# Gate and up products of a SwiGLU layer by Strassen's method: seven products for eight

## The chip, the cores and the metric

The kernel runs on 1 core of one Trainium2 chip. The metric is the device time of one execution in microseconds, the median of several runs. A profiled execution of the same kernel gives the trace. PE is TensorE (matmuls), DVE is VectorE, ACT is ScalarE, POOL is GpSimd, and SP is the engine whose queue issues the DMAs.

## The reference

A decoder block on 256 tokens with 2048 channels: two token mixers, merged, and then a dense SwiGLU layer with 5632 hidden columns. All is float32. Cut to what matters here:

```python
def reference(x, ...):
    h = _rms_norm(x, attn_norm)
    ...                                        # two mixers, merge, output projection
    x = x + mix @ w_out
    h2 = _rms_norm(x, ffn_norm)
    x = x + (jax.nn.silu(h2 @ w_gate) * (h2 @ w_up)) @ w_down
```

h2 is 256 x 2048, w_gate and w_up are 2048 x 5632, w_down is 5632 x 2048.

## The kernel before

Every large product is done in float32 precision with three matmuls. An operand is split in two: hi is its copy in the rounded type float32r (ACT, L107 or in the helper hilo), lo is what is missing (DVE subtracts hi from the value, L108 or in hilo). A product is then hi x hi + hi x lo + lo x hi (L122 to L124); a matmul takes a 128x128 stationary piece of the activation and 512 moving columns of the weight.

load_pair brings two k-tiles of a weight, 512 columns wide (a raw tile of 128x1024, 512 KB, in one DMA from SP's queue; the pool has four raw buffers), and splits it into whi and wlo (three buffers each). chunk_tok does one block of 512 columns: for each pair of k-tiles two k-tiles x two token tiles x three matmuls, 12 in all, into one PSUM bank per token tile; then it calls an evacuation. It is a generator: run steps it, and after each pair pumps a side task, if there is one.

The SwiGLU part goes over eleven column blocks (L1065 to L1067). For each, a gate chunk (8 pairs, 96 matmuls) is evacuated by evac_gate: silu of the product times the row's norm factor rs2 (ACT). Then comes an up chunk, evacuated by evac_up: product times rs2 times the silu (DVE, L1058), then four transposes on PE per token tile (transpose_hilo, L183) and a split of the transposed activation into act, which stays in SBUF. The norm's gain is already in h2T, its row factor rs2 is applied at the evacuations. Then w_down is streamed: four chunks of 44 k-tiles, with act as the stationary operand.

The order of the instructions on each engine is the tile framework's: it traces the program, orders by priority and an estimate of time, and sets the semaphores. A split of a later pair can so stand ahead of an evacuation that the program names first. Each engine works its own queue in order. Of POOL's work before, the select on Q (L712, 128x1024, one operand) and the small powers (L381) are mentioned below; Q and N belong to the delta rule mixer, where DVE also does small subtractions (L707, L708).

Of the kernel before, what the change touches and what calls it, by code (L numbers as in the profile page):

```python
# [16 lines left out]
P = 128  # L17
S = 256
# [25 lines left out]
def tile_hybrid_block(  # L44
# [36 lines left out]
    big = ctx.enter_context(tc.tile_pool(name="big", bufs=4))  # L81
    dram = ctx.enter_context(tc.tile_pool(name="dram", bufs=2, space=bass.MemoryType.DRAM))
    psm = ctx.enter_context(tc.tile_pool(name="psm", bufs=4, space=bass.MemoryType.PSUM))
    pss = ctx.enter_context(tc.tile_pool(name="pss", bufs=4, space=bass.MemoryType.PSUM))

# [10 lines left out]
    def sps():  # L96
        return pss.tile([P, 512], F32, tag="sd", name=nm("sd"))
# [81 lines left out]
    def transpose_hilo(src4, hi, lo, k0, t):  # L179
        """src4: four [P, P] pieces of a token-major tile, to k-tiles k0..k0+3 of hi and lo."""  # L180
# [112 lines left out]
    def narrow():  # L293
# [29 lines left out]
        # softplus(a) = max(a, 0) + log1p(exp(-|a|)), the log1p as 2 artanh(e / (2 + e))  # L323
# [9 lines left out]
        # the argument is at most 1/3, so terms to s^15 reach float32  # L333
# [53 lines left out]
    def normed_T(pst, hi, lo, gcol):  # L387
        """rms-norm of four heads side by side, transposed, times a gain by channel"""
# [209 lines left out]
    # merge-gate logits and the product of branch A wait in DRAM for the merge  # L598
# [46 lines left out]
    def conv_silu(st, ps, base, silu_out):  # L645
        """short causal convolution of four heads by channel, then silu"""
# [30 lines left out]
    # one-hot columns for the blocks' inverses: lane = 32 * column group + problem  # L677
# [8 lines left out]
    def gdn_prep(st, hg):  # L686
        """what hangs on the decay alone"""
# [52 lines left out]
    def gdn_q(st, hg):  # L740
# [22 lines left out]
        # the 32 x 32 blocks on the diagonal, a problem and eight of its columns to a lane  # L763
# [237 lines left out]
    fin = ctx.enter_context(tc.tile_pool(name="fin", bufs=1))  # L1001
    gain2 = fin.tile([P, D], F32, name="gain2", tag="gain2")
# [4 lines left out]
    x2 = fin.tile([P, NT, D], F32, name="x2")  # L1007
# [4 lines left out]
    ss2 = fin.tile([P, NT, 4], F32, name="ss2")  # L1012
# [17 lines left out]
    act = [[], []]  # L1030
    for q in range(2):
        for i in range(3):
            if i == 2:
                act[q].append(fin.tile([P, 12, S], F32R, name=f"act{q}{i}"))
            elif i == 1:
                act[q].append(fin.tile([P, 16, S], F32R, name=f"act{q}{i}"))
            else:
                act[q].append(big_tile(f"act{q}{i}", F32R))
    rs2 = fin.tile([P, NT], F32, name="rs2")
    sst = fin.tile([P, NT], F32, name="sst")  # L1040
# [7 lines left out]
    def evac_gate(c):
        def f(t, ps):
            sg[t] = fin.tile([P, 512], F32, tag="tmp", name=nm("sg"), bufs=6)  # L1050
            nc.scalar.activation(sg[t], ps, AF.Silu, scale=rs2[:, t : t + 1])

        return f

    def evac_up(c):
        def f(t, ps):
            a = sg[t]
            nc.vector.scalar_tensor_tensor(a, ps, rs2[:, t : t + 1], a, ALU.mult, ALU.mult)  # L1058
            k0 = 4 * c
            transpose_hilo(  # L1060
                [a[:, i * P : (i + 1) * P] for i in range(4)], act[0][k0 // 16], act[1][k0 // 16], k0 % 16, t
            )

        return f
# [51 lines left out]
```

## Time and profile before

| | us |
|---|---|
| median of 3 runs | 1974.59 |
| lowest, highest | 1973.98, 1975.04 |
| span of the profiled execution, first to last instruction | 1971.1 |
| PE busy in the span | 1946.4 |
| DVE, ACT, POOL busy | 1155.0, 928.4, 54.1 |

The span is that of one profiled execution; the runs' time also has what lies around it. Busy times count the time in which at least one instruction of an engine is under way. Matmuls overlap each other in the trace, so the duration of one is longer than the distance to the next. The weights that are streamed come to 355.76 MB read from HBM.

### The profile page before, as it was taken

Reading aid. Unit: us, or ns where it says so; the run is one execution under the profiler, and the core shown is the slowest. Engines: PE = TensorE matmul, PEld = TensorE weight load, DVE = VectorE, ACT = ScalarE, POOL = GpSimd, SP = SyncE. Lnnn points to the kernel's source line nnn. Section 1 sums busy time; section 2 is a strip of 40 time slices with the busy share of each in tenths; the row PEclk is TensorE's granted clock in tenths of the full one; section 3 lists DMA queues with packets and bytes.
Section 4 is the critical chain, followed back from the end, with each engine's and each line's share of the span. In section 5 each row is a group of like instructions: output and inputs, shape, how many; then the busy total and the mean of one; then the engine's idle time right before and its main releaser. Section 6 shows DMA issues by size and latency. Waiting matters only on the chain.

```text
span 1971.1 us, 27260 instructions
## 1 busy us (share of the span) xinstructions
PE 1946.4 (99%) x10485; PEld 1651.0 (84%) x10485; DVE 1155.0 (59%) x1715; ACT 928.4 (47%) x1377; POOL 54.1 (3%) x97
## 2 busy tenths in 40 slices
PE   8999999999999999999999999999999999999999
PEld 6878877876998998999987788888888888888887
DVE  5555766655468587687774665554455444544443
ACT  5434555555454554654543544444444444443333
POOL 0001000001000000100100000000000000000000
PEclk9999999999999999999999999999999999999999
DMA  8566545546767566566574965666666666656663
GB/s 231 170 183 193 161 129 162 170 149 200 217 173 203 169 178 198 158 193 166 153 200 157 333 201 183 191 192 183 191 191 186 191 191 191 191 185 201 201 202 130
DMA packets 207605, 367.04 MB, mean 186 GB/s; under 512 B 25473, under 2 KB 34546, under 8 KB 207090
## 3 DMA queue, kind: packets, MB, share of 16 engines
q1 hardware_dynamic: 207442, 365.28, 62.1%
q8 instruction: 82, 1.34, 0.3%
q14 instruction: 49, 0.40, 0.1%
q10 hardware_dynamic: 32, 0.01, 0.0%
HBM read 355.76 MB, written 9.45 MB: 185 GB/s over the span
## 4 chain that ended last, share of the span: by engine, by line
PE 96%; DMA 2%; DVE 1%; ACT 0%; SPq 0%; issue 0%; POOL 0%; ACTq 0%; POOLq 0%; DVEq 0%
PE mm L123 25%; PE mm L124 24%; PE mm L122 24%; PE mm L141 4%; PE mm L143 4%; PE mm L142 4%; PE sd L183 1%; PE sd L668 1%; PE sd L448 1%; PE sd L561 1%; DMA Q<-grow_d 1%; PE sd L748 1%; DMA raw<-in_w_branch_b_dram 1%; PE sd L567 1%; PE sd L568 0%; PE sd L267 0%
## 5 line engine op out<-in xcount | busy, mean ns | idle before, releaser
L108 DVE TENSOR_TENSOR wlo<-raw,whi 128x1024 fp32r<-128x1024 f32 x632 | 773.7, 1225 | 658.5 <-ACT whi L107 656.1
L107 ACT ACTIVATE whi<-raw 128x1024 fp32r<-128x1024 f32 x632 | 669.7, 1060 | 804.5 <-PE mm L124 674.4
L123 PE MATMUL mm<-wlo,hT_hi 128*128 128x512 f32 x704 | 276.7, 393 | 0.0
L124 PE MATMUL mm<-whi,hT_lo 128*128 128x512 f32 x704 | 276.5, 393 | 0.0
L124 PE MATMUL mm<-whi,h2T_lo 128*128 128x512 f32 x704 | 274.0, 389 | 0.0
L123 PE MATMUL mm<-wlo,h2T_hi 128*128 128x512 f32 x704 | 273.9, 389 | 0.0
L122 PE MATMUL mm<-whi,hT_hi 128*128 128x512 f32 x704 | 260.2, 393 | 0.0
L122 PE MATMUL mm<-whi,h2T_hi 128*128 128x512 f32 x704 | 249.9, 390 | 0.0
L143 PE MATMUL mm<-hT_hi,wlo 128*128 128x256 f32 x768 | 218.4, 285 | 0.0
L141 PE MATMUL mm<-hT_hi,whi 128*128 128x256 f32 x768 | 218.4, 285 | 0.0
L142 PE MATMUL mm<-hT_lo,whi 128*128 128x256 f32 x768 | 218.3, 284 | 0.0
L124 PEld LDWEIGHTS mm<-whi,hT_lo 128*128 128x128 f32 x704 | 132.3, 188 | 27.7 <-issue 1.1
L123 PEld LDWEIGHTS mm<-wlo,hT_hi 128*128 128x128 f32 x704 | 132.3, 188 | 27.5 <-issue 1.1
L124 PEld LDWEIGHTS mm<-whi,h2T_lo 128*128 128x128 f32 x704 | 132.2, 188 | 27.5
L122 PEld LDWEIGHTS mm<-whi,h2T_hi 128*128 128x128 f32 x704 | 132.2, 188 | 27.1
L123 PEld LDWEIGHTS mm<-wlo,h2T_hi 128*128 128x128 f32 x704 | 132.2, 188 | 27.0
L122 PEld LDWEIGHTS mm<-whi,hT_hi 128*128 128x128 f32 x704 | 132.1, 188 | 26.3 <-issue 0.2
L141 PEld LDWEIGHTS mm<-hT_hi,whi 128*128 128x128 f32 x768 | 147.2, 192 | 0.6
L142 PEld LDWEIGHTS mm<-hT_lo,whi 128*128 128x128 f32 x768 | 147.2, 192 | 0.2
L143 PEld LDWEIGHTS mm<-hT_hi,wlo 128*128 128x128 f32 x768 | 146.9, 192 | 0.4
L123 PE MATMUL mm<-wlo,act 128*128 128x512 f32 x352 | 138.5, 393 | 0.0
L124 PE MATMUL mm<-whi,act 128*128 128x512 f32 x352 | 138.4, 393 | 0.0
(288 smaller groups left out, 2247.7 us busy)
## 6 DMA issues: line engine op xcount, KB each, us to landing
raw<-in_w_in_dram SPq DMA_DIRECT2D x272, 512.0 KB, 3.7
raw<-in_w_gate_dram SPq DMA_DIRECT2D x88, 512.0 KB, 4.4
raw<-in_w_up_dram SPq DMA_DIRECT2D x88, 512.0 KB, 3.7
raw<-in_w_down_dram SPq DMA_DIRECT2D x88, 512.0 KB, 4.7
raw<-in_w_branch_a_dram SPq DMA_DIRECT2D x32, 512.0 KB, 4.7
raw<-in_w_branch_b_dram SPq DMA_DIRECT2D x32, 512.0 KB, 4.9
raw<-in_w_out_dram SPq DMA_DIRECT2D x32, 512.0 KB, 4.7
wc<-in_w_cmp_dram SPq DMA_DIRECT2D x16, 256.0 KB, 4.2
```

Of the source, the lines that this page charges most:

```text
L107: nc.scalar.activation(hi[:, :, :width], raw[:, :, :width], AF.Copy)
L108: nc.vector.tensor_tensor(lo[:, :, :width], raw[:, :, :width], hi[:, :, :width].bitcast(F32), ALU.subtract)
L122: nc.tensor.matmul(o, lhsT=sh, rhs=hi[:, j, :width], start=kt == 0, stop=False)
L123: nc.tensor.matmul(o, lhsT=sh, rhs=lo[:, j, :width], start=False, stop=False)
L124: nc.tensor.matmul(o, lhsT=sl, rhs=hi[:, j, :width], start=False, stop=kt == kts - 1)
L141: nc.tensor.matmul(o, lhsT=hi[:, j, ws], rhs=xh[:, kt, :], start=first, stop=False, skip_group_check=True)
L142: nc.tensor.matmul(o, lhsT=hi[:, j, ws], rhs=xl[:, kt, :], start=False, stop=False, skip_group_check=True)
L143: nc.tensor.matmul(o, lhsT=lo[:, j, ws], rhs=xh[:, kt, :], start=False, stop=last, skip_group_check=True)
L183: nc.tensor.transpose(pt[:, i * P : (i + 1) * P], s4, ident)
L448: nc.tensor.matmul(pc[:60, :P], lhsT=kp[:, l0 + l, :], rhs=wc[:, l, :], start=l0 + l == 0, stop=l0 + l == 31)
L561: nc.tensor.transpose(pt[:n, r * P : (r + 1) * P], pb[:, r, c0 : c0 + n], ident)
L567: nc.tensor.matmul(po, lhsT=wh, rhs=ph[:n], start=i == 0, stop=False)
```

## The change

Of the eleven column blocks, block 0 stays as it was, except that its activation is written to DRAM (act_d) and not transposed at once. Blocks 1 to 10 compute gate and up together by Strassen's method (in the Winograd form): the activation is cut into halves by token tile and by k (k-tiles 0 to 7 and 8 to 15), which gives a 2x2 matrix of pieces; gate's and up's two k-halves form the other 2x2 matrix. Seven products M1 to M7 take the place of eight. Each product still takes three matmuls for the split operands, and a step j (k-tiles j and j+8 of both weights) has 7 x 3 = 21 matmuls where chunk_tok has 24. There are 8 steps in a block. Seven PSUM banks hold M1 to M7.

The sums of the activation's pieces (S1 to S4) and the row factor rs2 are prepared once, by the side task factors, while block 0 runs: sums and products on POOL, splits on ACT and DVE. The sums of weight pieces (ta and tb, two 512-wide additions each) are made on POOL in every step and then split as the weights are. The seven products are put together at a block's end by DVE and ACT, silu and the product of gate and up included. Blocks 1 and 2 transpose their activation at once (act_r); the others write it to DRAM. During the first chunk of w_down the side task act_in reads it back, transposes and splits it. w_down's k-tiles are taken in the order of blocks 1, 2, 0, 3 to 10. PSUM and SBUF pools are closed and opened anew to make room.

```diff
--- before.py
+++ after.py
@@ -110,25 +124,26 @@
         )
         return hi, lo
 
-    def chunk_tok(w, c0, width, kts, stat, evac):
-        ps = [psm.tile([P, 512], F32, tag="mm", name=nm("mm")) for _ in range(NT)]
-        for k0 in range(0, kts, 2):
+    def chunk_tok(w, c0, width, kts, stat, evac, order=None):
+        ps = [mps() for _ in range(NT)]
+        pairs = order or list(range(0, kts, 2))
+        for n, k0 in enumerate(pairs):
             hi, lo = load_pair(w, k0, c0, width)
             for j in range(2):
-                kt = k0 + j
+                first, last = n + j == 0, j == 1 and n == len(pairs) - 1
                 for t in range(NT):
-                    sh, sl = stat(kt, t)
+                    sh, sl = stat(k0 + j, t)
                     o = ps[t][:, :width]
-                    nc.tensor.matmul(o, lhsT=sh, rhs=hi[:, j, :width], start=kt == 0, stop=False)
+                    nc.tensor.matmul(o, lhsT=sh, rhs=hi[:, j, :width], start=first, stop=False)
                     nc.tensor.matmul(o, lhsT=sh, rhs=lo[:, j, :width], start=False, stop=False)
-                    nc.tensor.matmul(o, lhsT=sl, rhs=hi[:, j, :width], start=False, stop=kt == kts - 1)
+                    nc.tensor.matmul(o, lhsT=sl, rhs=hi[:, j, :width], start=False, stop=last)
             yield
         for t in range(NT):
             evac(t, ps[t])
         yield
...
-    fin = ctx.enter_context(tc.tile_pool(name="fin", bufs=1))
+    fin = ctx.enter_context(tc.tile_pool(name="fin", bufs=1, side="right"))
...
-    h2T_hi = big_tile("h2T_hi", F32R)
-    h2T_lo = big_tile("h2T_lo", F32R)
+    h2T_hi = hp.tile([P, KD, S], F32R, name="h2T_hi")
+    h2T_lo = hp.tile([P, KD, S], F32R, name="h2T_lo")
...
+    NB = DFF // 512
+    big_cm.__exit__(None, None, None)
...
+    act_d = dram.tile([NB, NT, P, 512], F32, name="act_d", bufs=1)
...
+    A12, A11, A22, S1, S3, S2, S4 = range(7)
+    Fh = [fac.tile([P, 7, 2, P], F32R, name=f"Fh{g}") for g in range(4)]
+    Fl = [fac.tile([P, 7, 2, P], F32R, name=f"Fl{g}") for g in range(4)]
+
+    def tmp(n):
+        return fin.tile([P, 512], F32, tag="tmp", name=nm(n), bufs=6)
+
+    def factors():
+        dg = tmp("dg")
+        for t in range(NT):
+            nc.vector.tensor_scalar_mul(dg[:, t * P : (t + 1) * P], ident, rs2[:, t : t + 1])
+        one = tmp("one")
+        nc.vector.memset(one[:, :P], 1.0)
+        pr = sps()
+        nc.tensor.matmul(pr[:, :S], lhsT=one[:, :P], rhs=dg[:, :S], start=True, stop=True)
+        nc.scalar.activation(rsrow, pr[:, :S], AF.Copy)
+        yield
+        hv = h2T_hi.bitcast(F32).rearrange("p (h k) s -> p h k s", h=2)
+        lv = h2T_lo.bitcast(F32).rearrange("p (h k) s -> p h k s", h=2)
+        for g in range(4):
+            js = slice(2 * g, 2 * g + 2)
+            q = sw.tile([P, 4, 2, P], F32, tag="T", name=nm("q"), bufs=2)
+            for t in range(NT):
+                ts = slice(t * P, (t + 1) * P)
+                qt = q[:, 2 * t : 2 * t + 2]
+                nc.gpsimd.tensor_tensor(qt, hv[:, :, js, ts], lv[:, :, js, ts], ALU.add)
+                qf = qt.rearrange("p h k c -> p (h k) c")
+                nc.gpsimd.tensor_tensor(qf, qf, rsrow[:, ts].unsqueeze(1).to_broadcast([P, 4, P]), ALU.mult)
+            yield
+            sm = sw.tile([P, 4, 2, P], F32, tag="T", name=nm("sm"), bufs=2)
+            nc.gpsimd.tensor_tensor(sm[:, 0], q[:, 3], q[:, 2], ALU.subtract)
+            nc.gpsimd.tensor_tensor(sm[:, 1], q[:, 1], q[:, 3], ALU.subtract)
+            nc.gpsimd.tensor_tensor(sm[:, 2], q[:, 1], sm[:, 0], ALU.subtract)
+            nc.gpsimd.tensor_tensor(sm[:, 3], q[:, 0], sm[:, 2], ALU.subtract)
+            hilo(Fh[g][:, 0:3], Fl[g][:, 0:3], q[:, 0:3])
+            hilo(Fh[g][:, 3:7], Fl[g][:, 3:7], sm)
+            yield
...
-    for c in range(DFF // 512):
-        run(chunk_tok(w_gate, c * 512, 512, KD, stat_h2, evac_gate(c)))
-        run(chunk_tok(w_up, c * 512, 512, KD, stat_h2, evac_up(c)))
+    def evac_gate(t, ps):
+        sg[t] = tmp("sg")
+        nc.scalar.activation(sg[t], ps, AF.Silu, scale=rs2[:, t : t + 1])
+
+    def evac_up(t, ps):
+        nc.vector.scalar_tensor_tensor(sg[t], ps, rs2[:, t : t + 1], sg[t], ALU.mult, ALU.mult)
+        nc.sync.dma_start(act_d[0, t], sg[t])
+
+    side.append(factors())
+    run(chunk_tok(w_gate, 0, 512, KD, stat_h2, evac_gate))
+    run(chunk_tok(w_up, 0, 512, KD, stat_h2, evac_up))
+    drain()
+    hp_cm.__exit__(None, None, None)
+    close_banks()
+
+
+    late = ctx.enter_context(tc.tile_pool(name="late", bufs=1, side="right", reuse_waits="tile"))
+    act_r = [late.tile([P, 8, S], F32R, name=f"act_r{q}") for q in range(2)]
+    pst_cm = tc.tile_pool(name="pst", bufs=1, space=bass.MemoryType.PSUM, reuse_waits="tile")
+    pst = pst_cm.__enter__()
+    halves = {
+        "g": w_gate.rearrange("(h j p) c -> j p h c", h=2, p=P),
+        "u": w_up.rearrange("(h j p) c -> j p h c", h=2, p=P),
+    }
+
+    def split(src, n, pool, tag, bufs):
+        hi = pool.tile([P, 2, 512], F32R, tag=tag[0], name=nm(tag[0]), bufs=bufs)
+        lo = pool.tile([P, 2, 512], F32R, tag=tag[1], name=nm(tag[1]), bufs=bufs)
+        hilo(hi[:, :n], lo[:, :n], src[:, :n])
+        return hi, lo
+
+    def strassen_step(j, c, M, order, first, last):
+        raw = {}
+        for n in ("g", "u"):
+            raw[n] = stream.tile([P, 2, 512], F32, tag="raw", name=nm("raw"))
+            nc.sync.dma_start(raw[n], halves[n][j][:, :, c * 512 : (c + 1) * 512])
+        b21, b11, b22, b12 = raw["g"][:, 0], raw["g"][:, 1], raw["u"][:, 0], raw["u"][:, 1]
+        ta = sw.tile([P, 2, 512], F32, tag="T", name=nm("ta"), bufs=2)
+        nc.gpsimd.tensor_tensor(ta[:, 0], b11, b12, ALU.add)
+        nc.gpsimd.tensor_tensor(ta[:, 1], b22, b12, ALU.add)
+        tb = sw.tile([P, 2, 512], F32, tag="T", name=nm("tb"), bufs=2)
+        nc.gpsimd.tensor_tensor(tb[:, 0], ta[:, 0], b22, ALU.add)
+        nc.gpsimd.tensor_tensor(tb[:, 1], tb[:, 0], b21, ALU.add)
+        gh, gl = split(raw["g"], 2, stream, ("whi", "wlo"), 3)
+        uh, ul = split(raw["u"], 1, stream, ("whi", "wlo"), 3)
+        ah, al = split(ta, 2, sw, ("thi", "tlo"), 3)
+        bh, bl = split(tb, 2, sw, ("thi", "tlo"), 3)
+        moving = {
+            1: (A11, gh[:, 1], gl[:, 1]),
+            2: (A12, gh[:, 0], gl[:, 0]),
+            3: (S4, uh[:, 0], ul[:, 0]),
+            4: (A22, bh[:, 1], bl[:, 1]),
+            5: (S1, ah[:, 0], al[:, 0]),
+            6: (S2, bh[:, 0], bl[:, 0]),
+            7: (S3, ah[:, 1], al[:, 1]),
+        }
+        for m in order:
+            f, hi, lo = moving[m]
+            fh, fl = Fh[j // 2][:, f, j % 2], Fl[j // 2][:, f, j % 2]
+            nc.tensor.matmul(M[m], lhsT=fh, rhs=hi, start=first, stop=False)
+            nc.tensor.matmul(M[m], lhsT=fh, rhs=lo, start=False, stop=False)
+            nc.tensor.matmul(M[m], lhsT=fl, rhs=hi, start=False, stop=last)
+
+    def strassen_block(c):
+        M = {m: pst.tile([P, 512], F32, tag="M", name=nm("M"), bufs=7) for m in range(1, 8)}
+        for j in range(8):
+            order = (1, 2, 3, 5, 7, 6, 4) if j < 7 else (6, 1, 5, 3, 7, 4, 2)
+            strassen_step(j, c, M, order, j == 0, j == 7)
+        m1, v, x, y = tmp("m1"), tmp("v"), tmp("x"), tmp("y")
+        nc.scalar.activation(m1, M[1], AF.Copy)
+        nc.vector.tensor_tensor(v, M[6], m1, ALU.subtract)
+        nc.vector.tensor_tensor(x, M[5], v, ALU.add)
+        nc.vector.tensor_tensor(x, M[3], x, ALU.add)
+        nc.vector.tensor_tensor(v, v, M[7], ALU.subtract)
+        nc.vector.tensor_tensor(y, M[4], v, ALU.subtract)
+        nc.vector.tensor_tensor(m1, M[2], m1, ALU.add)
+        nc.vector.tensor_tensor(v, M[5], v, ALU.add)
+        nc.scalar.activation(m1, m1, AF.Silu)
+        nc.scalar.activation(y, y, AF.Silu)
+        nc.vector.tensor_tensor(x, m1, x, ALU.mult)
+        nc.vector.tensor_tensor(y, y, v, ALU.mult)
+        for t, a in enumerate((x, y)):
+            if c > 2:
+                nc.sync.dma_start(act_d[c, t], a)
+                continue
+            pt = pst.tile([P, 512], F32, tag="tr", name=nm("tr"), bufs=1)
+            for i in range(4):
+                nc.tensor.transpose(pt[:, i * P : (i + 1) * P], a[:, i * P : (i + 1) * P], ident)
+            ks, ts = slice(4 * c - 4, 4 * c), slice(t * P, (t + 1) * P)
+            hilo(act_r[0][:, ks, ts], act_r[1][:, ks, ts], pt.rearrange("p (k c) -> p k c", k=4))
+
+    for c in range(1, NB):
+        strassen_block(c)
+    pst_cm.__exit__(None, None, None)
+    sw_cm.__exit__(None, None, None)
+    fac_cm.__exit__(None, None, None)
+    open_banks()
+    actp = ctx.enter_context(tc.tile_pool(name="actp", bufs=1, reuse_waits="tile"))
+    rest = [0] + list(range(3, NB))
+    act_l = {c: [actp.tile([P, 4, S], F32R, name=f"act{q}_{c}") for q in range(2)] for c in rest}
+
+    def act_in():
+        for c in rest:
+            for t in range(NT):
+                a = tmp("a")
+                nc.sync.dma_start(a, act_d[c, t])
+                transpose_hilo([a[:, i * P : (i + 1) * P] for i in range(4)], act_l[c][0], act_l[c][1], 0, t)
+            yield
...
+    order = [4 * c + k for c in [1, 2] + rest for k in (0, 2)]
+    side.append(act_in())
     for c in range(4):
-        run(chunk_tok(w_down, c * 512, 512, KF, stat_act, evac_down(c)))
+        run(chunk_tok(w_down, c * 512, 512, KF, stat_act, evac_down(c), order), 1)
+    close_banks()
```

## Rows read from the trace of the kernel before

**Rows 1.** The page's first part: busy us, share of the span, instructions.
```profile
PE 1946.4 (99%) x10485; PEld 1651.0 (84%) x10485; DVE 1155.0 (59%) x1715; ACT 928.4 (47%) x1377; POOL 54.1 (3%) x97
```

**Rows 2.** Stretches: engines' busy time, granted PE clock, DMA share.
```profile
core 0: us, PE busy (x) PEld busy (x) DVE busy (x) ACT busy (x) POOL busy (x), PEclk, DMA share, GB/s
1085.00:1090.00 5.00, 4.99 (x12) 3.92 (x13) 0.82 (x2) 1.06 (x1) 0.00 (x0) 0.50 0.83 272
1277.20:1721.50 444.30, 444.30 (x2002) 368.80 (x2001) 222.24 (x202) 193.22 (x200) 0.00 (x0) 1.00 0.64 190
```

**Rows 3.** Up evacuations, two per block: ns min/median/max, first and last start.
```profile
L1058 DVE SCALAR_TENSOR_TENSOR sg<-mm,rs,sg x21: 739/743/746, 1277.2 to 1721.5; 128x512 f32<-128x512 f32 x21
```

**Rows 4.** Largest waits, 1277.2 to 1721.5 us: us together, times, longest.
```profile
ACT whi L107 <- PE mm L124: 226.6, 140, 1.7
DVE wlo L108 <- ACT whi L107: 215.6, 161, 2.1
...
```

**Rows 5.** Timeline of DVE, a block's end: start, us, xN merged [idle before].
```profile
1362.18 1.23 DVE L108 TENSOR_TENSOR wlo<-raw,whi 128x1024 fp32r<-128x1024 f32 x1 [1.49 <-ACT whi L107]
1364.90 1.23 DVE L108 TENSOR_TENSOR wlo<-raw,whi 128x1024 fp32r<-128x1024 f32 x1 [1.49 <-ACT whi L107]
1366.05 1.40 DVE L1058 SCALAR_TENSOR_TENSOR sg<-mm,rs,sg 128x512 f32<-128x512 f32 x2
...
1372.37 1.29 DVE L177 TENSOR_TENSOR act<-sd,act 128x512 fp32r<-128x512 f32 x2 [0.80 <-ACT act L176]
```

**Rows 6.** Timeline of PE at the transposes behind that block.
```profile
1371.10 1.04 PE L183 MATMUL sd<-ident,sg 128*128 128x128 f32 x8
1371.89 0.48 PE L122 MATMUL mm<-whi,h2T_hi 128*128 128x512 f32 x1
```

**Rows 7.** Groups by line, 1277 to 1722 us: busy us, mean ns; idle before.
```profile
L177 DVE TENSOR_TENSOR act<-sd,act 128x512 fp32r<-128x512 f32 x20 | 12.9, 686 | 7.9 <-ACT act L176 7.9
L107 ACT ACTIVATE whi<-raw 128x1024 fp32r<-128x1024 f32 x161 | 170.7, 1061 | 228.7 <-PE mm L124 228.2
L176 ACT ACTIVATE act<-sd 128x512 fp32r<-128x512 f32 x20 | 10.9, 596 | 14.2 <-PE sd L183 14.2
```

**Rows 8.** Timeline of DVE: two splits on end, POOL idle.
```profile
292.76 2.35 DVE L108 TENSOR_TENSOR wlo<-raw,whi 128x1024 fp32r<-128x1024 f32 x2
```

**Rows 9.** POOL's select on Q, all four: ns min/median/max.
```profile
L712 POOL TENSOR_SCALAR_AFFINE_SELECT Q<-Q x4: 1096/1100/1961, 475.2 to 827.0; 128x1024 f32<-128x1024 f32 x4
```

**Rows 10.** Timeline of POOL and DVE, the select of 1.96 us.
```profile
827.01 1.96 POOL L712 TENSOR_SCALAR_AFFINE_SELECT Q<-Q 128x1024 f32<-128x1024 f32 x1 [5.03 <-ACT Q L711]
...
826.80 3.25 DVE L108 TENSOR_TENSOR wlo<-raw,whi 128x1024 fp32r<-128x1024 f32 x2
```

**Rows 11.** Timeline of POOL and DVE, a select of 1.10 us.
```profile
475.24 1.10 POOL L712 TENSOR_SCALAR_AFFINE_SELECT Q<-Q 128x1024 f32<-128x1024 f32 x1 [9.99 <-ACT esc L715]
...
474.90 0.28 DVE L708 TENSOR_SCALAR Q<-Q,gcum 128x128 f32<-128x128 f32 x1
475.10 1.51 DVE L707 TENSOR_SCALAR N<-N,gcum 128x128 f32<-128x128 f32 x3
```

**Rows 12.** Timeline of POOL and DVE, a small power behind a split.
```profile
149.65 1.93 POOL L381 TENSOR_TENSOR rs<-ss,mhalf 128x4 f32<-128x4 f32 x1 [16.45 <-DVE ss L377]
...
149.48 1.23 DVE L108 TENSOR_TENSOR wlo<-raw,whi 128x1024 fp32r<-128x1024 f32 x1
```

**Rows 13.** Timeline of POOL, the same power with DVE idle at its start.
```profile
202.88 1.01 POOL L381 TENSOR_TENSOR rs<-ss,mhalf 128x4 f32<-128x4 f32 x1 [16.17 <-DVE ss L377]
```

**Rows 14.** DMA issues: count, KB each, median us from issue to landing.
```profile
raw<-in_w_gate_dram SPq DMA_DIRECT2D x88, 512.0 KB, 4.4
mA_d<-stg SPq DMA_DIRECT2D x8, 256.0 KB, 4.6
```

**Rows 15.** Timeline of PE ahead of the stretch with half clock.
```profile
1083.08 1.16 PE L668 MATMUL sd<-ident,y 128*128 128x128 f32 x4 [3.52 <-DVE y L871]
1085.02 0.80 PE L122 MATMUL mm<-whi,oTB_hi 128*128 128x512 f32 x1 [0.78 <-ACT oTB_hi L877]
```

More of the change, by code (lines that the diff above doesn't have):

```diff
@@ L80, in tile_hybrid_block, with open_banks, close_banks @@
     stream = ctx.enter_context(tc.tile_pool(name="stream", bufs=4))
-    big = ctx.enter_context(tc.tile_pool(name="big", bufs=4))
+    big_cm = tc.tile_pool(name="big", bufs=4)
+    big = big_cm.__enter__()
     dram = ctx.enter_context(tc.tile_pool(name="dram", bufs=2, space=bass.MemoryType.DRAM))
-    psm = ctx.enter_context(tc.tile_pool(name="psm", bufs=4, space=bass.MemoryType.PSUM))
-    pss = ctx.enter_context(tc.tile_pool(name="pss", bufs=4, space=bass.MemoryType.PSUM))
+    banks = {}
+    def open_banks():
+        for n in ("psm", "pss"):
+            cm = tc.tile_pool(name=n, bufs=4, space=bass.MemoryType.PSUM, reuse_waits="tile")
+            banks[n] = (cm, cm.__enter__())
+    def close_banks():
+        for n in ("pss", "psm"):
+            banks.pop(n)[0].__exit__(None, None, None)
+    open_banks()
     uid = [0]
@@ L96, in sps, with mps @@
     def sps():
-        return pss.tile([P, 512], F32, tag="sd", name=nm("sd"))
+        return banks["pss"][1].tile([P, 512], F32, tag="sd", name=nm("sd"))
+    def mps():
+        return banks["psm"][1].tile([P, 512], F32, tag="mm", name=nm("mm"))
     def load_pair(w, k0, c0, width):
@@ L130, in chunk_feat @@
     def chunk_feat(w, c0, evac, xh, xl):
-        ps = [psm.tile([P, 512], F32, tag="mm", name=nm("mm")) for _ in range(2)]
+        ps = [mps() for _ in range(2)]
         for k0 in range(0, KD, 2):
@@ L1000, in tile_hybrid_block @@
     scr.__exit__(None, None, None)
-    fin = ctx.enter_context(tc.tile_pool(name="fin", bufs=1))
-    gain2 = fin.tile([P, D], F32, name="gain2", tag="gain2")
+    fin = ctx.enter_context(tc.tile_pool(name="fin", bufs=1, side="right"))
+    x2 = fin.tile([P, NT, D], F32, name="x2")
+    ss2 = fin.tile([P, NT, 4], F32, name="ss2")
+    rs2 = fin.tile([P, NT], F32, name="rs2")
+    sst = fin.tile([P, NT], F32, name="sst")
+    rsrow = fin.tile([P, S], F32, name="rsrow")
+    hp_cm = tc.tile_pool(name="hp", bufs=1, side="right")
+    hp = hp_cm.__enter__()
+    gain2 = hp.tile([P, D], F32, name="gain2", tag="gain2")
     nc.sync.dma_start(gain2, ffn_norm.partition_broadcast(P).rearrange("p o d -> p (o d)"))
@@ L1027, in tile_hybrid_block @@
         run(chunk_tok(w_out, c * 512, 512, KD, stat_of(mixT_hi, mixT_lo), evac_out(c)))
[L1030 to L1040, printed above, removed]
+    NB = DFF // 512
+    big_cm.__exit__(None, None, None)
+    fac_cm = tc.tile_pool(name="fac", bufs=1, reuse_waits="tile")
+    fac = fac_cm.__enter__()
+    sw_cm = tc.tile_pool(name="sw", bufs=2, reuse_waits="tile")
+    sw = sw_cm.__enter__()
+    act_d = dram.tile([NB, NT, P, 512], F32, name="act_d", bufs=1)
     nc.vector.tensor_reduce(sst, ss2, AX.X, ALU.add)
@@ L1045, in tile_hybrid_block @@
     stat_h2 = stat_of(h2T_hi, h2T_lo)
     sg = {}
[L1048 to L1064, printed above, removed]
@@ L1070, in stat_act @@
     def stat_act(kt, t):
-        ts = slice(t * P, (t + 1) * P)
-        return act[0][kt // 16][:, kt % 16, ts], act[1][kt // 16][:, kt % 16, ts]
+        c, ts = kt // 4, slice(t * P, (t + 1) * P)
+        if c in act_l:
+            return act_l[c][0][:, kt % 4, ts], act_l[c][1][:, kt % 4, ts]
+        return act_r[0][:, kt - 4, ts], act_r[1][:, kt - 4, ts]
     def evac_down(c):
```

3 lines of the change are left out of this document (1 added, 2 removed).

## The prediction

> **What bounds the kernel now.** First the page's busy times: PE is busy for 99% of the span, and DVE, ACT and POOL for 59%, 47% and 3% [rows 1]. A busy PE alone proves little, so I took the stretch that is changed, from the first gate/up block's up evacuation to the eleventh's: ten blocks in 444.3 us, 44.43 us each, PE busy throughout at full clock, DVE at 222.2 us and ACT at 193.2 us, half idle, POOL at 0 [rows 2, 3]. The waits of that stretch then say who waits for whom: ACT waits for PE (the weight buffers come free as PE uses them), DVE waits for ACT, and PE, busy for all of it, waits for nobody [rows 2, 4]. So the stage is bound by the number of matmuls. One weight pair (12 matmuls) has a period of 2.72 us on DVE, from one split (the subtraction that makes wlo) to the next, so a matmul is 2.72 / 12 = 0.2267 us [rows 5]; the 393 ns of the page are overlapping times. The eight transposes of a block take 1371.89 - 1371.10 = 0.79 us of PE [rows 6]. Check: 192 x 0.2267 + 0.79 = 44.3 us.
>
> **What goes.** A step of the change puts 21 matmuls in the place of the 24 of two weight pairs (one of gate, one of up). Over 8 steps and 10 blocks, 240 matmuls fall away: 240 x 0.2267 = 54.4 us of the bounding engine. That is all that can be won. PE then needs 21 x 0.2267 = 4.76 us in a step. The transposes aren't saved; those of eight blocks and of block 0 move into the first down-projection chunk, at 0.79 us each as before.
>
> **What a step adds on ACT and DVE.** Before, 24 matmuls came with two splits of 128x1024. Now four pieces are split: g (1024), half of u (512), and the sums ta and tb (1024 each). ACT: 3 x 1.06 + 0.60 = 3.8 us [rows 7], below PE's 4.76. DVE: two splits on end take 2.35 us, the second 2.35 - 1.23 = 1.12 us after the first, say 1.13 [rows 8]; a 512-wide one 1.29 - 0.69 = 0.60 [rows 5, 7]. A step: 3 x 1.13 + 0.60 = 4.0 us. At the end of a block DVE has nine 512-wide operations (v, x, x, v, y, m1, v, and two products), 9 x 0.60 = 5.4 us. So DVE, half idle now, would alone have 8 x 4.0 + 5.4 = 37.4 us beside PE's 38.1 us per block: no slack left, before POOL does anything.
>
> **What a step adds on POOL, the term that decides.** Four additions of 128x512 with two operands. No large two-operand POOL row exists. The nearest is the select on Q, 128x1024 with one operand, 1.10 us [rows 9]: it reads as many elements as an addition of two 512-wide operands, so I take 1.10 us. Below, half of it (0.55, if only the 512 outputs count); above, half as much again (1.65) for the range, and twice (2.2, if each operand cost a 1024-wide pass) as a rival. [...] Four of them are 4.4 us, under PE's 4.76. If POOL ran freely beside DVE, this would be covered.
>
> It doesn't. At 827.01 the select took 1.96 us instead of 1.10: a DVE split had begun 0.21 us before it. The split behind it was held up in turn: the two splits together took 3.25 us instead of 2.35 [rows 8, 10]. At 475.24 three small DVE operations (0.28 us each) took 1.51 us under the select, and at 149.65 a tiny POOL operation took 1.93 us instead of 1.01 because a split was running [rows 11 to 13]. Both directions, then: a split and a POOL operation that reads SBUF run one after the other. One POOL operation of 1.10 us puts 3.25 - 2.35 = 0.90 us on DVE's chain (0.20 us are lost in start and end, where they overlap). A step on the shared resource is therefore 4.0 + 4 x 0.90 = 7.6 us: longer than PE's 4.76, and than the 5.44 us (24 matmuls) that the same work takes now. The two T buffers per step tie POOL to DVE (the next ta waits for the split of this one), but POOL has two sums to do while the other waits, so I expect one of the two always to run, and no further loss.
>
> **A block.** 8 x 7.6 + 5.4 = 66.2 us. Seven of the nine closing operations read one operand from PSUM; no row shows a POOL operation beside such a one. I take these as free of the conflict, so the next step's four additions run under them: 4 x 0.90 = 3.6 us back, 62.6 us. [...] DVE also has to wait for PE: from the last step's splits PE needs 4.76 us, then m1, v and the products, 4 x 0.60, follow: 7.2 instead of 5.4 us, at most 1.8 us more. Splits of the next block can stand ahead of the closing operations, as the split at 1364.90 stands ahead of the evacuation at 1366.05 [rows 5], so I take half: 63.5 us. Against 44.43 - 0.79 = 43.64 us now: +19.9 us a block, +199 us for ten.
>
> **The rest.** The factors (A sums) run beside block 0: sixteen POOL operations of 512 and sixteen of 256, 16 x 0.90 + 16 x 0.35 = 20 us on DVE's chain, and 8 us of splits, with DVE's 22.2 us a block make 50.2 us against 44.4: +6 us (0 to 12). The seams (first Strassen step, PSUM banks given over, first down pairs behind the last block's closing operations): +4 us (0 to 8). The activation's way over DRAM: 18 writes and 18 reads of 256 KB. The writes stand in SP's queue behind the two products, ahead of later weight loads; the four raw buffers (two steps, 15 us) cover a wait of at most one block end (7 us). The reads of block n come a pair or more ahead of use and land in about 4 us [rows 14]. In the first nine down pairs DMA has 1 MB per 12 x 0.2267 + 0.8 = 3.5 us, 300 GB/s, about the 272 of the densest stretch shown [rows 2]. Cost zero; uncovered it would be a few us in nine pairs, inside the 4 us.
>
> **The sum.** Span 1971.1 + 199 + 10 = 2180 us. The profiled span is 3.5 us below the runs' median of 1974.59, so 2180 + 3.5 = 2184 us (rounded up).
>
> **Rivals.** (1) No conflict, the faster side: the additions run beside the splits. Then PE bounds at 168 x 0.2267 = 38.1 us a block, with up to 3.5 us idle at its end (m1, v, products, next split), so 2 to 5.5 us less a block: -20 to -55 + 10, 1930 to 1965 us, middle 1947. It decides if the conflict of [rows 10] holds for the select alone and not for two-operand sums. Against: three different POOL and two DVE operations show it. For: none of the rows is a two-operand POOL operation of this size. (2) Cheap additions, 0.55 us: 0.35 us on the chain each, step 5.4, block 43.2 + 5.4 - 1.4 + 1.8 = 49.0 us, +54 + 10, 2038 us: slower still. Below that, 1965 to 2035 us, would need a conflict of part of the time only. (3) Dear additions: at 1.65 us, 1.45 on the chain, step 9.8, block about 80 us, 2350 us; at 2.2 us, step 12, block 96 us, 2508 us. (4) PE's clock falls because it idles a third of each step. After 3.52 and 0.78 us of idle time PE stood at half clock from 1085 on [rows 2, 15]; a matmul was then 0.427 us apart, a step 9.0 us, a block about 74 us, 2285 us. Against: idle time inside a step comes in pieces of about 1 us, as each split releases its 3 to 6 matmuls. At a block's end it may fall, but there PE has slack to make it up.
>
> **Chances.** Forecast with prices between 0.55 and 1.65 us: 0.74, 2035 to 2350, nearest 2184. Clock: 0.05, inside that range. Dear additions beyond 1.65: 0.05. Partial conflict: 0.03. No conflict: 0.13. The range 2035 to 2350 holds 0.79. A measurement of this kernel can tell about 0.2% (4 us) from no change. Faster 0.12 (no conflict), within 0.2% 0.02 (its poor end with the partial conflict), slower 0.86.
>
> **What would show it.** Right: in the Strassen stretch PE is busy about 60%, with waits of PE on the lo splits; DVE close to solid with splits of about 2 us mean instead of 1.23; POOL additions at about 2 us instead of 1.1; a block of about 63 us. The price: the shortest addition on POOL is 1.10 us. Wrong: splits that stay at 1.23 us beside POOL, PE above 90%, block of 40 us (rival 1); PEclk of 0.5 inside blocks (rival 4); additions well off 1.1 us at their shortest (rivals 2, 3).

## The result, and the profile after

The changed kernel takes 2241.9 us (median of 4), the kernel before 1974.3 us beside it: a ratio of 1.136, 95% interval 1.134 to 1.137. Its four executions lie within 0.8 us. It is slower, by 268 us, where 2184 us, 210 us more, was predicted. The range of 2035 to 2350 us holds the time.

The first part of the page of the changed kernel, the line that answers [rows 1]:

```profile
PE 2024.8 (90%) x10247; PEld 1601.5 (71%) x10247; DVE 1606.1 (72%) x1956; ACT 1064.1 (47%) x1556; POOL 745.9 (33%) x449
```

PE has 238 instructions less in the trace, near the 240 matmuls that were taken away, and POOL has 692 us of work more. The stretches of the changed kernel, to compare with [rows 2]: the Strassen blocks from first to last M matmul, block 0 ahead of them, the down-projection behind them, and eight steady blocks from one block's last product to another's:

```profile
core 0: us, PE busy (x) PEld busy (x) DVE busy (x) ACT busy (x) POOL busy (x), PEclk, DMA share, GB/s
1289.60:1983.70 694.10, 507.10 (x1698) 306.21 (x1698) 643.98 (x414) 316.45 (x355) 644.85 (x322) 0.95 0.43 128
1233.10:1289.60 56.50, 51.47 (x209) 39.69 (x208) 41.52 (x33) 26.48 (x32) 48.62 (x32) 0.94 0.50 147
1983.70:2240.40 256.70, 251.40 (x1129) 206.78 (x1127) 124.94 (x119) 100.27 (x105) 0.00 (x0) 0.99 0.62 198
...
1382.60:1933.10 550.50, 404.56 (x1356) 244.93 (x1356) 510.19 (x333) 251.69 (x284) 512.41 (x257) 0.95 0.44 129
```

A block takes 550.5 / 8 = 68.8 us, against 44.43 before. PE is busy for 73% of it; DVE and POOL for 93% each. Two engines at 93% don't look like one resource. But put their instructions' starts and ends together: from 1292.4 to 1980.3 us, nearly all of the ten blocks, there is no moment at which neither is under way (counted from the trace), and an instruction that is held up counts as busy: a split of 1024, 1.23 us in [rows 5], has a mean of up to 2.23 us in the groups below. Where the loss lies, 269 us of the profiled span: the ten blocks take 694.1 us instead of 444.4 (+249.7), block 0 with the factors 55.1 instead of 44.4 (+10.7, from its first matmul to the next block's), the down-projection 256.7 instead of 249.2 (+7.5, of which 9 x 0.79 = 7.1 us are the transposes that moved there), and what precedes all this +1.4.

The groups of the Strassen stretch of the changed kernel by line, 1300 to 1960 us; the columns are busy us, mean ns of one, then the engine's idle time before them in us and what ended it. L1144 to L1148 are the four additions, L191 and L192 the two halves of a split (ACT's copy hi, DVE's difference lo), L1185 and L1186 the two products at a block's end, L1182 one of the closing operations with an operand in PSUM:

```profile
L1145 POOL TENSOR_TENSOR ta<-raw 128x512 f32<-128x512 f32 x77 | 168.3, 2186 | 0.0
L1147 POOL TENSOR_TENSOR tb<-ta,raw 128x512 f32<-128x512 f32 x77 | 168.2, 2184 | 0.0
L1148 POOL TENSOR_TENSOR tb<-tb,raw 128x512 f32<-128x512 f32 x77 | 160.6, 2086 | 6.0
L1144 POOL TENSOR_TENSOR ta<-raw,raw 128x512 f32<-128x512 f32 x77 | 129.2, 1679 | 38.4 <-DVE tlo L192 38.4
...
L192 DVE TENSOR_TENSOR wlo<-raw,whi 128x1024 fp32r<-128x1024 f32 x78 | 173.6, 2226 | 12.5 <-ACT whi L191 12.3
L192 DVE TENSOR_TENSOR tlo<-ta,thi 128x1024 fp32r<-128x1024 f32 x77 | 145.7, 1892 | 3.0 <-ACT thi L191 1.2
L192 DVE TENSOR_TENSOR wlo<-raw,whi 128x512 fp32r<-128x512 f32 x77 | 123.5, 1604 | 0.5 <-ACT whi L191 0.5
L192 DVE TENSOR_TENSOR tlo<-tb,thi 128x1024 fp32r<-128x1024 f32 x77 | 122.3, 1588 | 31.0 <-ACT thi L191 30.9
L1186 DVE TENSOR_TENSOR y<-y,v 128x512 f32<-128x512 f32 x9 | 15.9, 1772 | 0.0
L1185 DVE TENSOR_TENSOR x<-m,x 128x512 f32<-128x512 f32 x9 | 10.6, 1178 | 0.0
L1182 DVE TENSOR_TENSOR v<-M,v 128x512 f32<-128x512 f32 x9 | 6.1, 679 | 0.0
```

The difference of 1024 that took 1.23 us in [rows 5] now has a mean of 2.23 us for whi and wlo (1.89 and 1.59 for those of the sums), with the same shape and types. The operation with one operand in PSUM (L1182) keeps its 0.68 us; the products, with both operands in SBUF, don't. The waits in the eight blocks: total us, times, longest us. L1165 and L1166 are matmuls of a step, PEld is PE's loading of the stationary piece:

```profile
ACT thi L191 <- POOL tb L1148: 153.3, 56, 3.4
PEld M L1166 <- DVE wlo L192: 75.6, 79, 2.1
PEld M L1165 <- ACT whi L191: 68.5, 71, 1.7
...
PE M L1166 <- DVE wlo L192: 40.6, 64, 1.7
PE M L1165 <- ACT whi L191: 38.1, 58, 1.3
```

In [rows 4] the arrow went from PE to ACT and on to DVE. Now PE waits for the splits, about as long for ACT's copies as for DVE's differences, ACT waits for POOL's sums, and POOL's own idle time (38.4 us above) is spent waiting for a split.

### The profile page after: what moved, and what is told of

Its sections match the earlier page's. It is cut to its first block, busy times and chain, and to the rows that moved or that the text cites. A ratio compares the mean times of both kernels' runs of the same rounds, so it can differ in the third digit from the quotient of the medians.

```text
span 2240.4 us, 27936 instructions
## 1 busy us (share of the span) xinstructions
PE 2024.8 (90%) x10247; PEld 1601.5 (71%) x10247; DVE 1606.1 (72%) x1956; ACT 1064.1 (47%) x1556; POOL 745.9 (33%) x449
## 4 chain that ended last, share of the span: by engine, by line
PE 65%; POOL 18%; DVE 9%; issue 5%; DMA 2%; ACT 1%; POOLq 0%; SPq 0%; ACTq 0%; DVEq 0%
PE mm L138 15%; PE mm L139 15%; PE mm L137 15%; POOL tb L1147 5%; POOL tb L1148 5%; PE mm L156 4%; PE mm L158 4%; PE mm L157 4%; DVE wlo L192 4%; POOL ta L1144 4%; POOL ta L1145 3%; DVE tlo L192 2%; PE sd L683 1%; DVE y L1186 1%; PE sd L463 1%
## 5 line engine op out<-in xcount | busy, mean ns | idle before, releaser
L122 DVE TENSOR_TENSOR wlo<-raw,whi 128x1024 fp32r<-128x1024 f32 x472 | 588.0, 1248 | 426.2 <-ACT whi L121 423.8
L121 ACT ACTIVATE whi<-raw 128x1024 fp32r<-128x1024 f32 x472 | 499.5, 1060 | 561.1 <-PE mm L139 433.3
L192 DVE TENSOR_TENSOR wlo<-raw,whi 128x1024 fp32r<-128x1024 f32 (+1 forms) x160 | 305.6, 1915 | 13.0 <-ACT whi L191 12.7
L191 ACT ACTIVATE thi<-tb 128x1024 fp32r<-128x1024 f32 x80 | 84.7, 1059 | 192.5 <-POOL tb L1148 192.5
L1145 POOL TENSOR_TENSOR ta<-raw 128x512 f32<-128x512 f32 x80 | 175.1, 2188 | 0.0
L1147 POOL TENSOR_TENSOR tb<-ta,raw 128x512 f32<-128x512 f32 x80 | 174.5, 2181 | 0.0
L1166 PE MATMUL M<-tlo,Fh 128*128 128x512 f32 x320 | 142.0, 444 | 31.1 <-DVE tlo L192 30.9
L1148 POOL TENSOR_TENSOR tb<-tb,raw 128x512 f32<-128x512 f32 x80 | 167.0, 2088 | 6.3
L191 ACT ACTIVATE whi<-raw 128x1024 fp32r<-128x1024 f32 (+1 forms) x160 | 133.3, 838 | 69.5 <-DMA raw<-in_w_gate_dram 41.3
L1165 PE MATMUL M<-thi,Fh 128*128 128x512 f32 x320 | 119.5, 442 | 44.8 <-ACT thi L191 44.5
L1166 PE MATMUL M<-wlo,Fh 128*128 128x512 f32 x240 | 108.2, 451 | 55.7 <-DVE wlo L192 54.7
L192 DVE TENSOR_TENSOR tlo<-ta,thi 128x1024 fp32r<-128x1024 f32 x80 | 151.3, 1891 | 3.1 <-ACT thi L191 1.2
L192 DVE TENSOR_TENSOR tlo<-tb,thi 128x1024 fp32r<-128x1024 f32 x80 | 126.8, 1585 | 32.1 <-ACT thi L191 32.1
```

Of the source, the lines that this page charges most:

```text
L121: nc.scalar.activation(hi[:, :, :width], raw[:, :, :width], AF.Copy)
L122: nc.vector.tensor_tensor(lo[:, :, :width], raw[:, :, :width], hi[:, :, :width].bitcast(F32), ALU.subtract)
L192: nc.vector.tensor_tensor(dst_lo, src, dst_hi.bitcast(F32), ALU.subtract)
L1147: nc.gpsimd.tensor_tensor(tb[:, 0], ta[:, 0], b22, ALU.add)
L1148: nc.gpsimd.tensor_tensor(tb[:, 1], tb[:, 0], b21, ALU.add)
L1166: nc.tensor.matmul(M[m], lhsT=fh, rhs=lo, start=False, stop=False)
```

## The experiments

A block below is a tenth of the time from the first to the last M matmul; for the changed kernel that is 69.4 us, 0.6 more than a steady block, since the first and the last block are in it. The runs that leave work out were executed once each, the last one ten times; those that move work to DVE and leave nothing out, twice. All runs have a kernel before beside them on the same chip, between 1973.3 and 1973.5 us.

**No sums.** POOL's additions are left out.

```diff
-        ta = sw.tile(...)
-        nc.gpsimd.tensor_tensor(ta[:, 0], b11, b12, ALU.add)
...
-        ah, al = split(ta, 2, sw, ("thi", "tlo"), 3)
-        bh, bl = split(tb, 2, sw, ("thi", "tlo"), 3)
+        ah, al = split(raw["u"], 2, sw, ("thi", "tlo"), 3)
+        bh, bl = split(raw["g"], 2, sw, ("thi", "tlo"), 3)
```

> The four weight sums of a step are left out: the pieces ta and tb are replaced by the raw weights, so POOL has nothing to do in a step; ACT, DVE and PE do the same number and sizes of operations. Theory (POOL and the DVE splits exclude each other): without POOL a block is bound by PE (168 x 0.2267 = 38.1 us) or DVE (37.4 us), 38 to 42 us instead of 68.8, the whole kernel 1930 to 1965 us, lo splits back to a mean of 1.23 us. Rival (the stage is slow for the longer chain of splits, the banks or PE's clock): block stays above 55 us, the whole above 2100 us.

Measured: 1977.2 us, a block 42.0 us, splits of 1024 back at a mean of 1.22 us. 265 us of the loss of 268 hang on the four additions of a step. The block is at the upper end of what was expected. The whole is 12 us above the range, a miss: block 0 took 60.5 us in this run, 5 us more than in the changed kernel with the same factors, and why wasn't settled.

**The same sums, made but not read.** POOL adds as in the changed kernel; what is split are the raw weights.

```diff
         ta = sw.tile(...)
         nc.gpsimd.tensor_tensor(ta[:, 0], b11, b12, ALU.add)
...
-        ah, al = split(ta, 2, sw, ("thi", "tlo"), 3)
-        bh, bl = split(tb, 2, sw, ("thi", "tlo"), 3)
+        ah, al = split(raw["u"], 2, sw, ("thi", "tlo"), 3)
+        bh, bl = split(raw["g"], 2, sw, ("thi", "tlo"), 3)
```

> POOL makes all four sums of a step as in the changed kernel, but nobody reads them: what is split in their place are the raw weights. So no step waits for POOL's result and POOL waits for no split. Theory (conflict over reading SBUF): the block stays at 66 to 70 us, the whole at 2215 to 2250 us, splits near 2 us, additions near 2.2 us. Rival (the chain from POOL's sum over ACT's copy and DVE's split back to POOL's buffer sets the time): the block falls to 38 to 42 us, the whole to 1930 to 1965 us.

Measured: 2241.75 us, a block 68.6 us. It differs from the run above only by POOL's additions, whose results nobody waits for, and it takes as long as the changed kernel. So the chain from POOL over ACT and DVE back to POOL's buffers isn't what sets the time; that rival falls. One tie is left: POOL still reads the raw buffers, so it could delay the loads. The stretch of eight blocks and a group of the splits:

```profile
1381.30:1934.70 553.40, 401.12 (x1354) 259.52 (x1353) 549.88 (x332) 247.25 (x282) 511.92 (x258) 0.92 0.40 128
...
L192 DVE TENSOR_TENSOR tlo<-raw,thi 128x1024 fp32r<-128x1024 f32 x153 | 320.0, 2119 | 0.0
```

DVE is busy for 549.9 of 553.4 us, with splits of 2.12 us that wait for nothing before they start. Late loads would show as idle time of DVE, and there is next to none.

**POOL writes but reads nothing.** Fills take the additions' place; the sums are left out.

```diff
-        nc.gpsimd.tensor_tensor(ta[:, 0], b11, b12, ALU.add)
...
+        for w in (ta, ta, tb, tb):
+            nc.gpsimd.memset(w.rearrange("p a c -> p (a c)"), 1.0)
```

> The four additions of a step are replaced by four fills of 128x1024 with ones, which write the same tiles but read nothing; a fill took 0.95 us before, so POOL is busy about 3.8 us in a step, and the chain from POOL over ACT and DVE back to POOL's buffer is kept. Theory (the conflict is over reads): splits stay at 1.23 us, block 38 to 45 us, the whole 1930 to 2000 us. Rival (any POOL work of that length holds DVE up): 4 x 0.75 us more per step, block about 62 us, the whole about 2165 us.

Measured: 1999.1 us, a block 45.4 us, 0.4 above what was expected. The groups of this run, 1300 to 1730 us:

```profile
L192 DVE TENSOR_TENSOR wlo<-raw,whi 128x1024 fp32r<-128x1024 f32 x78 | 95.4, 1223 | 20.5 <-ACT whi L191 20.4
L192 DVE TENSOR_TENSOR tlo<-ta,thi 128x1024 fp32r<-128x1024 f32 x77 | 94.2, 1223 | 15.9 <-ACT thi L191 15.7
...
L1146 POOL MEMSET tb<- 128x1024 f32 x153 | 146.2, 955 | 95.9 <-DVE tlo L192 91.2
L1146 POOL MEMSET ta<- 128x1024 f32 x153 | 146.2, 955 | 44.8 <-DVE tlo L192 40.4
```

Splits at 1.22 us and fills at 0.955 us, both at the length they have alone, though POOL is at work two thirds of the time; with POOL's additions the splits took 2.12 us. What held DVE's splits up was POOL's reading of SBUF, not its being at work or its writing. A block takes 3.4 us more than without sums; POOL's idle time here ends with splits (91.2 and 40.4 us), so the chain of dependencies is the likely reason, which wasn't tried apart.

**The sums on DVE,** all four; nothing is left out.

```diff
-        nc.gpsimd.tensor_tensor(ta[:, 0], b11, b12, ALU.add)
+        nc.vector.tensor_tensor(ta[:, 0], b11, b12, ALU.add)
...
```

> The four sums of a step are made on DVE instead of POOL, nothing else is changed. DVE then has 4.0 + 4 x 0.60 = 6.4 us a step and 5.4 to 7.2 us at a block's end. Theory: block 56.6 to 58.4 us, DVE-bound, the whole 2118 to 2138 us, faster than the changed kernel by about 5% and still slower than the kernel before. Rival (POOL's sums cost less than DVE's would, since they overlap at least in part): the whole at or above 2242 us.

Measured: 2132.9 us, 1.081 (1.078 to 1.084) of the kernel before, a block 58.5 us. The stretch of eight blocks of this run, from one block's last product to another's:

```profile
1367.40:1830.40 463.00, 371.22 (x1355) 243.40 (x1354) 460.90 (x589) 248.30 (x284) 0.00 (x0) 0.97 0.48 153
```

DVE is busy for 460.9 of 463.0 us: this one is plainly DVE-bound. Additions on end start 0.60 us apart. So DVE's own work without sums is about 58.5 - 32 x 0.60 = 39.3 us a block, and an addition on POOL costs (69.4 - 39.3) / 32 = 0.94 us net, on DVE 0.60. POOL as a helper is dearer than no helper.

**Two of the four sums on DVE** (those of tb).

```diff
-        nc.gpsimd.tensor_tensor(tb[:, 0], ta[:, 0], b22, ALU.add)
-        nc.gpsimd.tensor_tensor(tb[:, 1], tb[:, 0], b21, ALU.add)
+        nc.vector.tensor_tensor(tb[:, 0], ta[:, 0], b22, ALU.add)
+        nc.vector.tensor_tensor(tb[:, 1], tb[:, 0], b21, ALU.add)
```

> The two sums of ta stay on POOL, the two of tb are made on DVE. DVE's own work in a block is 58.5 - 32 x 0.60 = 39.3 us by the run with all sums on DVE. Theory A (each POOL addition costs the shared path the same, (68.8 - 39.3) / 32 = 0.92 us net): 39.3 + 16 x 0.60 + 16 x 0.92 = 63.6 us a block, the whole about 2185 us, in the middle between the two kernels. Theory B (a POOL addition costs 1.09 us where it meets a split, and some 5 per block are hidden under the closing operations, whatever their number): 39.3 + 9.6 + 11 x 1.09 = 60.9 us, the whole about 2160 us. Rival (a chain of dependencies): no change or slower.

Measured: 2194.8 us (ratio 1.112, 1.109 to 1.115), a block 64.7 us, 10 us above theory A and 35 above theory B. (64.7 - 39.3 - 9.6) / 16 = 0.99 us per POOL addition. Theory B's fixed number of additions that hide falls; each costs about the same. Why it came out 10 us above theory A wasn't settled.

**Additions of half the width.** As the run with unread sums; half of each sum is left out.

```diff
+        cut = slice(0, 256)
-        nc.gpsimd.tensor_tensor(ta[:, 0], b11, b12, ALU.add)
+        nc.gpsimd.tensor_tensor(ta[:, 0, cut], b11[:, cut], b12[:, cut], ALU.add)
...
```

> As the run whose sums nobody reads (2241.75 us), but each POOL addition covers 256 columns instead of 512; the other halves of the sums are left out. One such operation took 0.73 us alone among the factors, against 1.27 us for 512. Theory A (what an addition costs goes with its own length): 0.92 x 0.73 / 1.27 = 0.53 us net, block 39.3 + 32 x 0.53 = 56.3 us, the whole about 2118 us. Rival (a fixed cost for each change of hands between POOL and DVE): the whole stays above 2180 us.

Measured: 2082.3 us, a block 52.6 us, (52.6 - 39.3) / 32 = 0.42 us an addition. No fixed cost per change of hands: that rival falls. Theory A missed by 36 us: the cost falls faster than in proportion to the length. The section on the prediction has a working that fits both.

**The select in place of the addition.** The row that the price was taken from [rows 9], four times a step; the sums are left out.

```diff
-        nc.gpsimd.tensor_tensor(ta[:, 0], b11, b12, ALU.add)
...
+        for w, r in ((ta, "g"), (ta, "u"), (tb, "g"), (tb, "u")):
+            nc.gpsimd.affine_select(
+                out=w.rearrange("p a c -> p (a c)").rearrange("p (e c) -> p e c", e=8),
+                in_=raw[r].rearrange("p a c -> p (a c)").rearrange("p (e c) -> p e c", e=8),
+                compare_op=ALU.is_ge, fill=0.0, base=0, pattern=[[0, 8], [1, P]], channel_multiplier=-1,
+            )
```

> As the run whose sums nobody reads, but each addition is replaced by the select of the kernel before, 128x1024 with one operand, the row from which the price of an addition was taken (1.10 us alone, 0.90 us on DVE's chain). The sums are left out. If only that price was off (an addition of two 512-wide operands takes 1.27 us alone and not 1.10), a select costs 0.17 to 0.19 us less than an addition: 32 x 0.18 = 5.8 us less a block, 62.8 us, the whole about 2184 us, the time that was predicted. If what was off lies elsewhere (less is hidden, more waits), the whole stays at 2225 us or above.

Measured: 2185.2 us, a block 63.0 us; predicted for the changed kernel were 2184 us and 63.5 us. With the operation that the prediction priced, its block holds to 0.5 us. That the whole holds to 1 us is in part luck: the ten blocks took 630.5 us, 4.5 less than ten times 63.5, and block 0 59.9 us where 50.2 stood. The lines of the select in this run and of an addition in the changed kernel (ns min/median/max):

```profile
L1146 POOL TENSOR_SCALAR_AFFINE_SELECT ta<-raw x160: 1088/2036/2078, 1291.9 to 1916.7; 128x1024 f32<-128x1024 f32 x160
```

```profile
L1145 POOL TENSOR_TENSOR ta<-raw x80: 1268/2268/2353, 1293.6 to 1972.5; 128x512 f32<-128x512 f32 x80
```

Alone (the shortest of each), 1.09 against 1.27 us.

**All sums on DVE, the factors' too:** every sum and product of factors and strassen_step.

```diff
-                nc.gpsimd.tensor_tensor(qt, hv[:, :, js, ts], lv[:, :, js, ts], ALU.add)
+                nc.vector.tensor_tensor(qt, hv[:, :, js, ts], lv[:, :, js, ts], ALU.add)
...
```

> All sums on DVE, those of the activation's pieces (factors) too. Against the run with the weight sums on DVE (2133 us) only block 0 changes: it took 55.3 us there, with DVE at 22.2 us of its own, 8 us of splits and 32 POOL operations that exclude it. On DVE the 16 operations of 512 and 16 of 256 take 16 x 0.60 + 16 x 0.33 = 15 us, in all 45 us against PE's 44.4: block 0 at 45 to 48 us, the whole 2122 to 2126 us. Rival (block 0 is long for another reason, such as the order of the side task): no change.

Measured: 2124.8 us (ratio 1.077, 1.074 to 1.080), block 0 at 46.1 us instead of 55.1. The conflict is there too: of the 10.7 us that the factors cost with POOL, 9.0 are gone; DVE's own sums cost 1.7.

**What the method could give with free sums.** No weight sums, as in the first run, and the factors on DVE.

```diff
-        nc.gpsimd.tensor_tensor(ta[:, 0], b11, b12, ALU.add)
...
-                nc.gpsimd.tensor_tensor(qt, hv[:, :, js, ts], lv[:, :, js, ts], ALU.add)
+                nc.vector.tensor_tensor(qt, hv[:, :, js, ts], lv[:, :, js, ts], ALU.add)
...
```

> No weight sums at all (they are left out, raw weights are split in their place) and the factors' sums on DVE: what Strassen's method would give here if its weight sums cost nothing and POOL did nothing. Against the run without sums (1977.22 us, block 42.0 us, block 0 60.7 us) block 0 falls to about 46 to 48 us: the whole 1961 to 1966 us, some 0.5% under the kernel before. Of the 54.4 us that 240 matmuls are worth, about 10 would be left, since DVE's own 39.3 us a block stands where PE's 38.1 should. Rival (DVE is not what holds the block at 42.0 us in that run, but POOL's part in block 0 alone): block near 38 us, the whole below 1930 us.

Measured: 1967.0 us, ratio 0.9976 (0.9963 to 0.999), a block 42.5 us, block 0 46.1 us. This is 1 us above the expected range; the ten executions lie between 1965.1 and 1976.4 us. Of 54.4 us that 240 matmuls are worth, some 7 are left, even with sums that cost nothing. A stretch of this run:

```profile
1380.00:1680.00 300.00, 281.86 (x1192) 223.76 (x1191) 271.95 (x291) 213.46 (x248) 0.00 (x0) 0.98 0.66 211
```

PE at 94%, DVE at 91%, neither full. DVE's work and PE's are near equal, and each waits now and then for ACT and ACT for weights (PE's longest waits name ACT's copies, and ACT's name the raw weights' DMAs). How the 42.5 us part between these wasn't settled. With sums that must be made, no version of this kind was found that beats the kernel before: the best was 2124.8 us.

## Why the prediction was right, and where it was off

**The bound.** Right. PE was the bound and the stage had only 54.4 us to win; DVE was to have no slack left. Without POOL a block stood at 42 us, with DVE and PE both above 90%.

**The conflict.** Right, and nearly the whole loss hangs on it: with sums unread 2241.75 us, without sums 1977.2 us. That one of DVE and POOL would always run, with no further loss in the dependencies, held as well: there is no gap between the two in the steady blocks. Rival 1, no conflict, falls; so does the conflict for part of the time only. The rows before were thinner than the prediction reads them. [rows 11 to 13] show two kinds of POOL operation, not three, and in [rows 13] a split began 0.10 us behind the small power and took its usual time:

```profile
202.98 1.23 DVE L108 TENSOR_TENSOR wlo<-raw,whi 128x1024 fp32r<-128x1024 f32 x1 [0.25 <-ACT whi L107]
```

A split held the power up in [rows 12], but this power didn't hold a split up. That POOL holds a split up rested on the select alone; for large additions the experiments showed it.

**The price of an addition, the step that was mis-sized.** The prediction took 1.10 us from the select, on the argument that it reads as many elements. Alone an addition took 1.27 us (0.73 us for 256 columns). By steady blocks, 68.8 us here and 463.0 / 8 = 57.9 with the sums on DVE, DVE's own work is 57.9 - 32 x 0.60 = 38.7 us and the 32 additions put 30.1 us on a block, 0.94 each. The prediction had 28 x 0.90 = 25.2 us, 0.79 each. That is 4.9 of the 5.3 us by which 63.5 was too low; DVE's own work, 38.7 where 37.4 + 0.9 stood, is the other 0.4. Over ten blocks this makes 53 of the 58 us that the forecast missed. In the run with the select itself a block took 63.0 us.

**What hides under the closing operations.** Right in kind. DVE and POOL at a block's end in the changed kernel, timeline of either:

```profile
1505.81 1.28 POOL L1144 TENSOR_TENSOR ta<-raw,raw 128x512 f32<-128x512 f32 x1
...
1505.25 0.67 DVE L1181 TENSOR_TENSOR m<-M,m 128x512 f32<-128x512 f32 x1
1505.85 0.68 DVE L1178 TENSOR_TENSOR x<-M,x 128x512 f32<-128x512 f32 x1
1506.44 0.67 DVE L1179 TENSOR_TENSOR v<-v,M 128x512 f32<-128x512 f32 x1
```

An addition at 1.28 us, its length alone, beside operations with one operand in PSUM at their 0.67 us: neither held the other up. The products at a block's end, with both operands in SBUF, had means of 1.18 and 1.77 us in the changed kernel (L1185, L1186). The splits, with both operands in SBUF too, took 2.12 us beside additions that read SBUF (the run with unread sums) and 1.22 us beside fills that only write it.

How much hides can be estimated. The four additions (3.6 us) that the prediction takes back were an assumption, and no run shows that number. In the steady blocks POOL was under way for 4.35 us a block beside such operations (counted from the trace), 4.35 / 1.27 = 3.4 additions where the prediction hid four. With the prediction's 0.20 us of overlap taken off the others, (32 - 3.4) x (1.27 - 0.20) = 30.6 us a block, against 30.1 measured. The same working gives 24.7 us for the select (24.7 measured), 13.7 for the half-width additions (14.0) and 15.1 for two sums on POOL (15.6); their steady blocks took 63.35, 52.74 and 63.86 us, counted from the traces as above. So the form of the prediction's term held, and its main wrong entry was the length of an addition.

**The rest.** Factors +6 us (0 to 12): +10.7, and 1.7 on DVE; in the four runs that split raw weights with POOL at work on the factors, block 0 took 58.5 to 60.5 us, which wasn't explained. Seams +4 (0 to 8): the down-projection grew by 0.4 us beyond the moved transposes, and the first and the last Strassen block together took 694.1 - 550.5 = 143.6 us, 6 more than two steady ones. DRAM detour: nothing, right, as far as those 0.4 us tell. PE busy was foreseen at about 60% and was 73%. That counts overlapping times; the matmuls themselves, 168 x 0.2267 = 38.1 us of 68.8, are 55%. The clock (rival 4): 0.95 granted on the mean of the ten blocks, which is about 69 of 694 us at the half clock that [rows 2] show (0.50) and the rest at the full one (counted from the trace). It didn't set the time: with unread sums 0.92 was granted, DVE was busy for 549.9 of 553.4 us, and the whole took the same. Rivals 2 and 3 carry 1.8 us a block for DVE's wait at the end where the forecast carries 0.9; with 0.9 the range would start 9 us lower, which changes nothing here.

## What to carry to other kernels

Before work is moved to POOL, look in the trace for a large POOL operation that reads SBUF beside a DVE operation with two SBUF operands: if either is longer there than alone (here a split of 1024 took up to 2.23 us instead of 1.23, an addition up to 2.19 instead of 1.27, by their means), count the two engines as one for such work; the helper then costs most of its own length, here more (0.94 us) than the same addition on DVE (0.60 us). Take that length from the same operation: the row of another one was 0.17 us off, and the forecast with it. Two engines at 93% each can be one resource; their joint timeline tells, and an experiment with results that nobody reads separates it from a dependency. When saved matmuls are paid for with splits and sums, add up the other engines' work per block first: here DVE stood at PE's bound even with free sums.

## What the runs showed of the hardware

The exclusion cost less than a POOL operation's own length: 0.42 us for one of 0.73, 0.74 us ((63.0 - 39.3) / 32) for one of 1.09, 0.94 us for one of 1.27, each about 0.33 us less. By the estimate above 0.20 us of it is overlap at the change of hands and the rest is what hides under operations with a PSUM operand; no run changed the two one at a time. A two-operand addition of 2 x 512 elements took 0.18 us longer alone than a one-operand select of 1024 (1.27 and 1.09), so elements read alone don't set its length.
